# A sum of positive parts along rows: SyncE holds back its third and later loads until its first load has landed

## The chip, the cores and the metric

The kernel runs on one core of a Trainium2 chip. Five engines matter in different measure here: SyncE issues every transfer, ScalarE (ACT in the profile) and VectorE (DVE) compute, GpSimd (POOL) only sets four constants before the work begins, and TensorE does nothing. Transfers are carried by 16 DMA engines that all serve one queue. The metric is the time of one execution on the device, in microseconds (us); lower is better.

## The reference

The input has 32 x 512 rows of 1024 fp32 numbers, 64 MiB in all. Each row is cut at zero and summed.

```python
def reference(x: np.ndarray) -> np.ndarray:
    relu_x = np.maximum(x, 0)
    return np.sum(relu_x, axis=-1).astype(np.float32)
```

The result is 16,384 numbers, 64 KiB.

## The kernel before

The 16,384 rows are dealt to 128 partitions, 128 rows to each, in three regions (`REGIONS`, line 8): 1 row per partition, then 111, then 16. Within a region the rows of one partition are neighbours in memory. `xv` and `ov` (lines 45 to 49) are the views of input and output by region. A row of one partition is 4 KB, so "one row of each partition" is a load of 512 KB.

**Buffers.** `buf` has room for three buffers (`NB`) of 16 rows per partition (`BIG`), 8 MiB each. Big chunk `c` goes to buffer `c % 3`. There are seven big chunks, 0 to 6, and then 16 rows per partition of tail, cut into loads of 8, 4 and 2 rows and four pieces of the last two rows. Chunk 0 is the only one that is fetched by two loads (`CHUNKS`, line 9): first one row of each partition (512 KB, region 0), then 15 rows (7680 KB, region 1). Chunks 1 to 6 are one load of 16 rows each.

**SyncE's order (lines 85 to 123).** SyncE issues the loads in the order of the chunks, and the order is written out by hand. The two loads of chunk 0 are moved in the instruction list ahead of SyncE's arrival at the barrier with which all engines begin (lines 79 to 84, 95 to 97). Behind the barrier come chunks 1 and 2, with nothing to wait for, and from chunk 3 on a wait at line 87 until VectorE is through with the buffer that is to be refilled. The same wait stands ahead of the tail's loads. After those SyncE waits for results and issues the three stores. A semaphore `s_in[c]` counts 16 for each load that has landed; chunk 0's two loads share `s_in[0]`, so that its consumers wait for 32 (`16 * len(CHUNKS[c])`, lines 140 and 152).

**ScalarE and VectorE (lines 137 to 169).** For chunks 0 to 5 ScalarE cuts rows at zero in place in groups (`ACT_STEPS`), raising `s_act`, and VectorE sums the groups that ScalarE has finished (`DVE_STEPS`, line 160), raising `s_dve`, which frees the buffer. In chunk 0 this is one ScalarE instruction over all 16 rows and three reduces on VectorE. In chunks 4 and 5 some rows are left out of this pairing, and each engine does cut and sum of a row in a single instruction (`on_act`, `on_dve`, lines 126 to 132). Chunk 6 and the tail are done in that way throughout, with ScalarE and VectorE taking turns by rows (lines 173 to 185). The last row pair is cut at the element `CUT` and its pieces are gathered by sums in `seam` (lines 187 to 203). The output's last part is stored once both engines are done (line 207).

ScalarE needs its function table loaded ahead of its first ACTIVATE. No line of the kernel before asks for it; the compiler puts it in, and the profile shows it under line 145.

Of the kernel before, what the change touches and what calls it, by code (L numbers as in the profile page):

```python
# [8 lines left out]
CHUNKS = [[(0, 0, 1), (1, 0, 15)]] + [[(1, 16 * c + 15, 16)] for c in range(6)]  # L9
# [7 lines left out]
def bass_relu_sum_kernel(  # L17
# [16 lines left out]
    AF = mybir.ActivationFunctionType  # L34
# [21 lines left out]

    n_in = NBIG + len(TAIL) + 3
    s_in = [nc.alloc_semaphore(f"s_in{i}") for i in range(n_in)]
    s_act = nc.alloc_semaphore("s_act")
    s_dve = nc.alloc_semaphore("s_dve")  # L60
    s_fact = nc.alloc_semaphore("s_fact")
# [8 lines left out]
    sp, act, dve = nc.sync, nc.scalar, nc.vector  # L70
# [12 lines left out]
        if ins.engine == mybir.EngineType.SP and type(ins).__name__ == "InstDrain"  # L83
    )
    for c in range(NBIG + 1):
        if c >= NB:
            sp.wait_ge(s_dve, done[c - NB])
        if c < NBIG:
            i = 0
            for g, j, n in CHUNKS[c]:  # L90
                sp.dma_start(  # L91
                    out=buf[:, c % NB, i : i + n, :], in_=xv[g][:, j : j + n, :]
                ).then_inc(s_in[c], 16)
                i += n
                if c == 0:
                    code.insert(arrival, code.pop())
                    arrival += 1
# [28 lines left out]
    def on_act(t, acc):  # L126
        return act.activation(t, t, AF.Relu, accum_out=acc)  # L127

    def on_dve(t, acc):
        return dve.tensor_scalar(  # L130
            out=t, in0=t, scalar1=0.0, scalar2=None, op0=ALU.max, op1=ALU.add, accum_out=acc
        )

    def row(c, i):
        return buf[:, c % NB, i, :], res[:, c * BIG + i : c * BIG + i + 1]

    k = 0
    for c in range(NTWO):
        alone = BIG - sum(ACT_STEPS[c])
        act.wait_ge(s_in[c], 16 * len(CHUNKS[c]))  # L140
        r = 0
        ready = []
        for n in ACT_STEPS[c]:
            t = buf[:, c % NB, r : r + n, :]
            act.activation(t, t, AF.Relu).then_inc(s_act, 1)  # L145
            k += 1
            ready += [k] * n
            r += n
        for i in range(BIG - alone // 2, BIG):
            on_act(*row(c, i))  # L150
        if alone:
            dve.wait_ge(s_in[c], 16 * len(CHUNKS[c]))
            for i in range(BIG - alone, BIG - alone // 2):
                on_dve(*row(c, i))
        r = seen = 0
        for n in DVE_STEPS[c]:
            if ready[r + n - 1] > seen:
                seen = ready[r + n - 1]
                dve.wait_ge(s_act, seen)
            dve.tensor_reduce(  # L160
                out=res[:, c * BIG + r : c * BIG + r + n],
                in_=buf[:, c % NB, r : r + n, :],
                axis=X,
                op=ALU.add,
            ).then_inc(s_dve, 1)
            r += n
        if c == 1:
            dve.wait_ge(s_dve, done[c])
            dve.transpose(out=turned[:, :], in_=res[:, 0:32]).then_inc(s_turn, 1)  # L169
# [1 line left out]

    j0 = NBIG * BIG
    for c in range(NTWO, NBIG):
        act.wait_ge(s_in[c], 16 * len(CHUNKS[c]))
        dve.wait_ge(s_in[c], 16 * len(CHUNKS[c]))
        for i in range(BIG):
            ins = (on_act if i % 2 else on_dve)(*row(c, i))
            if i >= BIG - 2:
                ins.then_inc(s_fact if i % 2 else s_fdve, 1)
# [58 lines left out]
```

## Time and profile before

| what | value |
|---|---|
| median of 3 runs | 160.77 us |
| lowest and highest of them | 160.72 and 160.92 us |
| span of the profiled execution, first to last instruction | 159.4 us |
| VectorE busy | 120.6 us (76%) |
| ScalarE busy | 101.5 us (64%) |
| data queue, share of 16 DMA engines over the span | 98.1% |
| bytes read from HBM | 67.11 MB |

The page gives no whole time for the profiled execution, so its span stands beside the median of the runs that were timed. A span counts from the first instruction, here SyncE's first load, to the last. In the profile "SPq" is SyncE as it issues transfers; an issue is not counted as busy time of an engine, and its landing comes later. In a timeline a row gives its start, its length, the engine, the line, the operation and its tiles, and in brackets the idle time ahead of it and what ended that. In the table of stretches each row has the stretch, its length, the busy time of VectorE, ScalarE and GpSimd with their counts, the granted TensorE clock, the mean busy share of the 16 DMA engines and the GB/s that they moved. A packet is counted in a short stretch when it begins, so that shares over 1 are possible there.

### The profile page before, as it was taken

The page shows a single profiled execution, that of the slowest core. Times are in us where ns is not written, and L with a number is a line of the kernel's source. Part 1 is how long each engine was busy: PE and PEld are TensorE (multiplying, and loading weights), DVE is VectorE, ACT ScalarE, POOL GpSimd, SP SyncE. Part 2 cuts the span into 40 slices and gives each one's busy share as a digit, 9 for nine tenths or more (in the row PEclk, how much of TensorE's full clock was granted, in tenths as well). Part 3 has the DMA queues.
Part 4 walks back from the last instruction along what each step waited for, and adds up shares of the span by engine and source line. Part 5 has one row for each costly group of instructions (what it writes and reads, how often), then busy time and mean ns, then how long its engine had stood idle before and what let it go on. Part 6 is the DMA issues. An engine that isn't in the chain of part 4 may idle for free.

```text
span 159.4 us, 150 instructions
## 1 busy us (share of the span) xinstructions
DVE 120.6 (76%) x59; ACT 101.5 (64%) x54; POOL 0.2 (0%) x4
## 2 busy tenths in 40 slices
DVE  0000000009999999999999999999999999898995
ACT  3000059980799708996099941999329980496975
POOL 0000000000000000000000000000000000000000
DMA  9997996996996997989979969969969979798994
GB/s 378 493 401 339 493 526 263 526 526 263 526 493 296 526 444 345 526 378 411 526 312 477 526 263 526 526 263 526 526 263 526 444 345 526 321 469 374 417 400 142
DMA packets 2457, 67.18 MB, mean 421 GB/s; under 512 B 536, under 2 KB 792, under 8 KB 1176
## 3 DMA queue, kind: packets, MB, share of 16 engines
q1 hardware_dynamic: 2456, 67.18, 98.1%
q14 instruction: 1, 0.01, 0.0%
HBM read 67.11 MB, written 0.07 MB: 421 GB/s over the span
## 4 chain that ended last, share of the span: by engine, by line
DVE 55%; DMA 34%; ACT 9%; SPq 2%; issue 0%
DVE res L160 54%; DMA buf<-in_x_dram 34%; ACT buf L145 9%; SPq L101 1%; SPq L112 1%; DVE buf L130 0%; DVE seam L130 0%; SPq L91 0%; DVE turned L169 0%
## 5 line engine op out<-in xcount | busy, mean ns | idle before, releaser
L160 DVE TENSOR_REDUCE res<-buf 128x4 f32<-128x4096 f32 (+3 forms) x18 | 99.4, 5596 | 35.5 <-ACT buf L145 35.5
L145 ACT ACTIVATE buf<-buf 128x7168 f32<-128x7168 f32 (+5 forms) x13 | 80.4, 6233 | 46.1 <-DMA buf<-in_x_dram 46.1
L127 ACT ACTIVATE buf<-buf 128x1024 f32<-128x1024 f32 (+2 forms) x19 | 19.0, 999 | 8.9 <-DMA buf<-in_x_dram 8.9
L130 DVE TENSOR_SCALAR_CACHE_REDUCE buf<-buf 128x1024 f32<-128x1024 f32 (+2 forms) x19 | 20.7, 1143 | 1.7 <-DMA buf<-in_x_dram 1.6
L127 ACT ACTIVATION_READ_ACCUMULATOR buf<-buf 128x1 f32 x19 | 3.6, 188 | 0.0
L145 ACT ACT_TABLE_LOAD x1 | 1.3, 1283 | 1.3 <-PEq L223 1.3
L130 DVE DVE_READ_ACCUMULATOR buf<-buf 128x1 f32 x19 | 1.6, 84 | 0.0
L130 DVE TENSOR_SCALAR_CACHE_REDUCE seam<-seam 128x258 f32<-128x258 f32 x1 | 0.4, 421 | 0.0
L127 ACT ACTIVATE seam<-seam 128x114 f32<-128x114 f32 x1 | 0.3, 300 | 0.1
L169 DVE STREAM_TRANSPOSE turned<-res 128x32 f32<-128x32 f32 x1 | 0.2, 211 | 0.0
L127 ACT ACTIVATION_READ_ACCUMULATOR seam<-seam 128x1 f32 x1 | 0.2, 186 | 0.0
L223 POOL MEMSET const-bfloat16-1.0<- 128x1 bf16 x1 | 0.1, 101 | 0.0
L223 POOL MEMSET const-uint8-127<- 128x1 uint8 x1 | 0.1, 101 | 0.0
L223 POOL MEMSET const-float32-0.0<- 128x1 f32 x1 | 0.1, 98 | 0.2 <-issue 0.2
L223 POOL MEMSET const-float32-1.0<- 128x1 f32 x1 | 0.1, 98 | 0.0
L130 DVE DVE_READ_ACCUMULATOR seam<-seam 128x1 f32 x1 | 0.1, 82 | 0.0
## 6 DMA issues: line engine op xcount, KB each, us to landing
buf<-in_x_dram SPq DMA_DIRECT2D x1, 7680.0 KB, 21.1
buf<-in_x_dram SPq DMA_DIRECT2D x1, 4096.0 KB, 25.3
buf<-in_x_dram SPq DMA_DIRECT2D x1, 2048.0 KB, 29.9
buf<-in_x_dram SPq DMA_DIRECT2D x1, 1024.0 KB, 31.9
buf<-in_x_dram SPq DMA_DIRECT2D x1, 512.0 KB, 3.3
buf<-in_x_dram SPq DMA_DIRECT2D x1, 456.0 KB, 32.5
buf<-in_x_dram SPq DMA_DIRECT2D x1, 256.0 KB, 32.7
seam<-in_x_dram SPq DMA_DIRECT2D x1, 184.0 KB, 32.6
```

Of the source, the lines that this page charges most:

```text
L101: sp.dma_start(out=buf[:, tb, r : r + n, :], in_=xv[-1][:, r : r + n, :]).then_inc(s_in[NBIG + i], 16)
L112: sp.dma_start(out=flat[:, lo:hi], in_=rows[:, lo:hi]).then_inc(s_in[NBIG + len(TAIL) + k], 16)
L127: return act.activation(t, t, AF.Relu, accum_out=acc)
L130: return dve.tensor_scalar(out=t, in0=t, scalar1=0.0, scalar2=None, op0=ALU.max, op1=ALU.add, accum_out=acc)
L145: act.activation(t, t, AF.Relu).then_inc(s_act, 1)
L160: dve.tensor_reduce(out=res[:, c * BIG + r : c * BIG + r + n], in_=buf[:, c % NB, r : r + n, :], axis=X, op=ALU.add,).then_inc(s_dve, 1)
L169: dve.transpose(out=turned[:, :], in_=res[:, 0:32]).then_inc(s_turn, 1)
L223: nc = _bacc.Bacc("TRN2", target_bir_lowering=False, num_devices=1)
```

## The change

Load one of chunk 0, the single row of each partition, gets a semaphore of its own, `s_row`. SyncE waits for it ahead of chunk 1, and so ahead of every later load. ScalarE's table load is now asked for by name, ahead of a wait for `s_row` that stands in front of all of ScalarE's work. As each `s_in[c]` now counts one load only, its consumers wait for 16.

```diff
+    s_row = nc.alloc_semaphore("s_row")
...
     for c in range(NBIG + 1):
+        if c == 1:
+            sp.wait_ge(s_row, 16)
         if c >= NB:
             sp.wait_ge(s_dve, done[c - NB])
...
-                ).then_inc(s_in[c], 16)
+                ).then_inc(s_in[c] if i or c else s_row, 16)
...
+    act.preload_act_table(AF.Relu)
+    act.wait_ge(s_row, 16)
     k = 0
     for c in range(NTWO):
         alone = BIG - sum(ACT_STEPS[c])
-        act.wait_ge(s_in[c], 16 * len(CHUNKS[c]))
+        act.wait_ge(s_in[c], 16)
...
         if alone:
-            dve.wait_ge(s_in[c], 16 * len(CHUNKS[c]))
+            dve.wait_ge(s_in[c], 16)
...
     for c in range(NTWO, NBIG):
-        act.wait_ge(s_in[c], 16 * len(CHUNKS[c]))
-        dve.wait_ge(s_in[c], 16 * len(CHUNKS[c]))
+        act.wait_ge(s_in[c], 16)
+        dve.wait_ge(s_in[c], 16)
```

## The prediction

> **What bounds the kernel now.** I read the page's head and its table of DMA queues first, then the table of stretches cut at the landings of the big loads, then the chain of work that ended last, then the timeline of ScalarE and SyncE and the idle gaps of VectorE.
>
> ```profile
> span 159.4 us, 150 instructions
> DVE 120.6 (76%) x59; ACT 101.5 (64%) x54; POOL 0.2 (0%) x4
> q1 hardware_dynamic: 2456, 67.18, 98.1%
> ```
>
> The one data queue keeps its 16 engines busy for 98.1% of the span; VectorE is busy for 76%. The stretches (us, DVE, ACT, POOL busy, PE clock, DMA share, GB/s) say where that holds:
>
> ```profile
> 21.60:40.90 19.30, 5.40 (x2) 13.86 (x1) 0.00 (x0) 1.00 1.00 435
> 40.90:60.30 19.40, 19.40 (x4) 13.95 (x2) 0.00 (x0) 1.00 1.00 432
> 60.30:79.60 19.30, 19.27 (x6) 13.95 (x2) 0.00 (x0) 1.00 1.00 435
> ```
>
> From 21.6 us on, an 8 MB load takes one stretch of 19.3 to 19.4 us whatever the engines do: VectorE works 5.4 us of one and all of the next, and the rate stays. The chain that ended last seems to tell something else:
>
> ```profile
> 0.45 21.14 DMA buf<-in_x_dram
> 21.61 13.87 ACT buf L145
> 35.50 34.59 DVE res L160 x6
> 70.33 51.73 DVE res L160 x9
> 122.07 0.33 SPq L101
> 124.39 32.60 DMA buf<-in_x_dram
> ```
>
> It walks back from the last landing to the instruction that released its issue, VectorE's work. But a load issued at 124.4 that lands at 157.0, 32.6 us for 128 KB, was queueing behind other loads. The queue, not VectorE, is the bound. The waits by line confirm it from the consumers: both wait for data at each stage, and VectorE's wait is never over 0.5 us.
>
> ```profile
> ACT buf L145 <- DMA buf<-in_x_dram: 46.1, 6, 19.1
> DVE buf L130 <- DMA buf<-in_x_dram: 1.6, 4, 0.5
> ```
>
> The start is the only stretch where the queue is not yet full; the timelines of SyncE and ScalarE show it:
>
> ```profile
> 1.27 0.33 SPq L91 DMA_DIRECT2D buf<-in_x_dram  x1
> 1.27 1.28 ACT L145 ACT_TABLE_LOAD   x1 [1.27 <-PEq L223]
> 21.61 13.86 ACT L145 ACTIVATE buf<-buf 128x16384 f32<-128x16384 f32 x1 [19.06 <-DMA buf<-in_x_dram]
> 40.97 13.95 ACT L145 ACTIVATE buf<-buf 128x7168 f32<-128x7168 f32 x2 [5.50 <-DMA buf<-in_x_dram]
> buf<-in_x_dram SPq DMA_DIRECT2D x1, 7680.0 KB, 21.1
> buf<-in_x_dram SPq DMA_DIRECT2D x1, 512.0 KB, 3.3
> ```
>
> SyncE issues load one (512 KB) at 0.00, two (7680 KB) at 0.45, three at 1.27, four at 1.65. Load one lands at 3.3 us. Load two keeps the queue until 21.6, and load three lands at 40.9, one full stretch later.
>
> **The change, step by step.** The sum is made against the profiled execution: its span of 159.4 us. The page gives no whole time for that execution, so I set the median of 160.77 beside it; the 1.4 us between them lies outside the first and last instruction, where no step of the change acts, and is carried over.
>
> Load three waits (line 86). Load one has landed at 3.32 us. SyncE's wake-up after a releaser costs 0.03 us (VectorE's reduce ends at 52.84, the load it releases is issued at 52.86). So load three is issued at about 3.35 instead of 1.27, 2.1 us later. From the first issue to the first bytes is 1.0 us (DMA share 0.00 from 0 to 1 us), up to 1.4 us on the last engine by the trace's packet records. Load three's descriptors are there by 3.35 + 1.4 = 4.8 us, and the queue reaches them when load two is through, about 21.0. The cover is load two's 18 us of queued bytes, with 16 us left over. Were that cover gone, the step would cost the 2.1 us whole. Value 0; the row that fits best is load five, issued at 52.86 while load four runs and needed at 60.3, with no loss in stretches either side.
>
> What is queued behind the waiting instruction: load four (1.65 to about 3.73, needed at 40.9), then the wait for VectorE's three reduces of buffer 0 (52.84 us, so 49 us away). ScalarE waits for loads three and four only at 40.97 and 60.31. Cost 0.
>
> The Trainium skill, page "DMA: Bandwidth & Descriptors", section "Rules for kernel authors", speaks against this change: issue a DMA early and wait late, so that its fixed cost (about 2.0 us there) overlaps. By that rule two late loads with bare fixed costs would make 160.77 + 4.0 = 164.8; the trace's stretches after 40.9 us, where every load is issued late, show none of it, so the sum goes by them.
>
> ScalarE's part: a wait on the new semaphore and an explicit table load. The wait is over at 3.3 us and the first ACTIVATE is released at 21.6, so it has 18.3 us of cover. The table load is the one that already runs from 1.27 to 2.55 and stays ahead of the wait. If it ran after the first landing it would end at 3.35 + 1.28 = 4.6: still 0. The dropped count of 32 on a shared semaphore becomes 16 on each of two: same moment, 21.6. The one extra semaphore adds no instruction on any engine's row of work. 0.
>
> What the move may shift is contention. Descriptors of loads three and four now reach the engines after load one, not beside it.
> - The gain is at most what stage one loses. In the packet records 10 of the 16 engines have one 4 KB packet of load one at 0.25 to 0.34 us instead of 0.16, between 1.74 and 2.24 us: up to 0.18 on one engine. Load two takes 21.59 - 3.32 = 18.27 us; 15/16 of a stretch of 19.35 is 18.14, so 0.13 is lost there. Together 0.31.
> - The loss: two issues beside the running 60 KB packets. At 122.1 to 125.3 us seven loads are issued, and the 64 KB packets then in flight take 0.05 and 0.03 us over their 2.42: 0.08 for seven, 0.02 for two. Worst row: the first 60 KB packets, up to 0.21 over their 2.27, twice: 0.42.
> - Value: load five's issue, which changes two of 16 packets by 0.016 us and stretches by 0.02 us; that is the same kind of load at the same place in a running load. The gain I put at the same 0.02, since packets at 5 and 7.4 us, long after the last issue, are also up to 0.28 late, so the early stalls do not need these issues. Both ends go into the range.
>
> Sum: 0 (load three) + 0 (load four and SyncE) + 0 (ScalarE) - 0.02 + 0.02 = 0. Span 159.4, time 160.77 us. A difference of 0.2%, 0.32 us, is about what a measurement of this kernel can tell from no change (the three runs lie within 0.20).
>
> **The rivals.**
> *Stage one gets cleaner.* If the queued descriptors cause the early stalls, the 0.31 above comes back: 160.46, still inside the bound. To pass it, the skew of the engines must shrink too: load one's 16 engines land from 2.81 to 3.32, and the last load's still from 156.98 to 157.44, so the last engine's late start is paid at the end. With half of that 0.51 also gone: 160.77 - 0.31 - 0.25 = 160.2. For it: that the skew persists for 154 us. Against it: the engines' first packets start 0.35 us apart before load three is issued, and the change does not touch that.
>
> *The late issues disturb load two.* This one ends slower: loads three and four meet 16 engines in the middle of 60 KB packets, and each costs the last engine the worst row, 0.21: 160.77 + 0.42 = 161.19. It decides from 0.16 us per load on. For it: the packets of 2.5 us, in flight as the descriptors of the old issues came, are the long ones. Against it: load five's 0.016 us and the tail's 0.01 per load.
>
> *ScalarE's table is loaded twice,* once more behind the 21.6 us landing. Then ScalarE and VectorE run 1.28 us late. VectorE ends its reduces at 137.3 + 1.28 = 138.6, and its waits for data, 0.42, 0.51 and 0.24 us, and 0.15 more ahead of 154.84, absorb 1.32: 160.77. Loads five to eight and the tail are issued 1.28 later; the tightest is load five, at 54.1 + 1.4 = 55.5 for a queue that is free at 60, with 4.5 us to spare. No change either.
>
> *The wait never binds.* It would need load one to have landed by 1.27; it lands at 3.3. Then 160.77 as well.
>
> **How the numbers follow.** No measurable change, with either harmless rival: 0.80, its own range 160.55 to 161.0 from the spread of the runs (0.20) round the median. Cleaner start beyond 0.32 us: 0.10, as half of it needs a skew that the change does not reach. Disturbed load two beyond 0.32 us: 0.10, as it needs ten times load five's row. Faster, same, slower: 0.10, 0.80, 0.10. The range goes from 160.45, the whole early loss regained, to 161.1, most of the worst row twice; the two rivals' tenths lie outside it.
>
> **What the changed profile would show.** Load three's issue at 3.35 instead of 1.27; load four's at 3.7; the first ACTIVATE still at 21.6 and the second at 40.97; stretches of 19.35 unchanged; one table load before 3 us. Wrong would be: the first ACTIVATE moved by more than 0.1 us, earlier (the stalls did come from the queued issues) or later (the late issues disturb). A gap in the DMA share near 21 us would mean that issue to first bytes is far longer under load than 1.4 us. A stretch other than 19.35 later on would mean the engines' order or skew sets the rate, which nothing here shows.

## The result and the profile after

The changed kernel is slower by a fifth of a per cent: 161.16 us (median of 22 runs, 160.76 to 161.53) against 160.80 us (22 runs, 160.72 to 161.03), a ratio of 1.0019 with a 95% interval of 1.0013 to 1.0024. No change was predicted, and 161.16 also lies above the range's end of 161.1.

The profile of the changed kernel shows none of this. Head, data queue, and the stretches between the landings of the big loads (same columns as before):

```profile
span 159.4 us, 151 instructions
q1 hardware_dynamic: 2456, 67.18, 98.0%
```

```profile
21.60:40.90 19.30, 5.31 (x2) 13.86 (x1) 0.00 (x0) 1.00 1.00 435
40.90:60.30 19.40, 19.40 (x3) 13.95 (x2) 0.00 (x0) 1.00 1.00 432
60.30:79.60 19.30, 19.27 (x6) 13.95 (x2) 0.00 (x0) 1.00 1.00 435
```

The span is 159.4 us again and the stretches are the same. One thing is new: 151 instructions instead of 150. The timelines of SyncE and ScalarE show the change at its place:

```profile
3.33 0.33 SPq L94 DMA_DIRECT2D buf<-in_x_dram  x1
1.26 1.28 ACT L140 ACT_TABLE_LOAD   x1 [1.26 <-PEq L228]
21.70 13.86 ACT L150 ACTIVATE buf<-buf 128x16384 f32<-128x16384 f32 x1 [19.16 <-DMA buf<-in_x_dram]
40.99 13.95 ACT L150 ACTIVATE buf<-buf 128x7168 f32<-128x7168 f32 x2 [5.43 <-DMA buf<-in_x_dram]
```

Load three is issued at 3.33 instead of 1.27 and the second chunk is taken up at 40.99 instead of 40.97. The first ACTIVATE starts 0.09 us later. The chain of work shows the new instruction just ahead of it, a ScalarE instruction of its own for one of the two waits:

```profile
21.64 0.02 ACTq L145
21.65 0.05 issue
21.70 13.87 ACT buf L150
```

The waits of the consumers (engine, line, releaser; us in total, times, longest) show that this does not reach the end: VectorE's wait for data is 1.6 us in total, as before:

```profile
ACT buf L150 <- DMA buf<-in_x_dram: 46.1, 6, 19.2
DVE buf L133 <- DMA buf<-in_x_dram: 1.6, 5, 0.5
```

So I looked at what each run has outside its span. Every run lists its time and its span, the latter to 0.1 us. In the runs of the kernel before on the next chip (35 of them) the time less the span is 1.31 to 1.42 us, mean 1.365. In the 22 runs of the changed kernel it is 1.40 to 1.97, mean 1.67: nine are at 1.40 to 1.46, thirteen at 1.71 to 1.97. The spans have a mean of 159.45. **The 0.3 us lie outside the first and last instruction.** The profiled execution is one of the nine, with 160.83 us.

The trace also holds the semaphore events behind the last instruction: a first closing barrier, the reset of the semaphores, and a second barrier. The profile's page does not print them, and the events name no engine: a barrier is read from nine updates of one semaphore, which come in the same pattern ahead of the program. In ns from the first event after the end, the second barrier reads

```
kernel before:   987 1021 1059 1103 1126 | 1223 1262 1296 1343
changed kernel:  992 1074 1112 1155 1179 | 1277 1315 1350 1396
```

I read the first five as the engines' arrivals and the rest as the way back. The second arrival comes 82 ns after the first instead of 34, and everything behind it is late by the same 48 ns. That is the 0.04 us which even a short execution has: with the trace's spans, which are given to the nanosecond, the profiled executions of this program length are at 1.40 to 1.42 outside, those of the length before (e3 to e5 below) at 1.36 to 1.38.

### The profile page after: what moved, and what is told of

It reads as the page before. It is cut to its first block, busy times and chain, and to the rows that moved or that the text cites. A ratio compares the mean times of both kernels' runs of the same rounds, so it can differ in the third digit from the quotient of the medians.

```text
span 159.4 us, 151 instructions
## 1 busy us (share of the span) xinstructions
DVE 120.6 (76%) x59; ACT 101.5 (64%) x54; POOL 0.2 (0%) x4
## 4 chain that ended last, share of the span: by engine, by line
DVE 55%; DMA 34%; ACT 9%; SPq 2%; issue 0%; ACTq 0%
DVE res L165 54%; DMA buf<-in_x_dram 34%; ACT buf L150 9%; SPq L104 1%; SPq L115 1%; DVE buf L133 0%; DVE seam L133 0%; SPq L94 0%; DVE turned L174 0%; ACTq L145 0%
```

## The experiments

All were timed beside the kernel before on the same chip; e1 to e4, e5 to e8, f1 to f4 and the g's each had a chip of their own. A result gives the median time, the ratio to the kernel before with its 95% interval, and "outside", which is the time less the span, as a mean over the runs. A figure in ns is the second arrival in the second closing barrier, counted from the first, in the profiled execution. Theory A puts the time inside the program (A1: SyncE's late issues; A2: ScalarE's wait). B puts it outside, by the extra semaphore. L puts it outside, by the length of ScalarE's program. W holds that it takes the wait for the row at ScalarE's start.

**The changed kernel once more** (e1).

> The changed kernel once more, as the yardstick for the others. The runs shown so far have 161.16 us against 160.80, yet spans of 159.3 to 159.6 on both sides. If the time was added inside the program (theory A: the two late issues disturb load two, or ScalarE's extra wait delays the start), a profile with a long time must show a first ACTIVATE later than 21.70 by 0.3 us or more. If it is added outside the first and last instruction (theory B), the span stays at 159.4 to 159.5 while the time is 161.0 to 161.3.

160.92 us, ratio 1.0009 (1.0000 to 1.0017). Outside 1.48 against 1.365: two of 12 runs at 1.72 and 2.0, the others at 1.38 to 1.46. The span's mean is 159.49 against 159.48. The late arrival is there again (82 ns). The time is outside the program, which speaks against A in both forms; how many executions are long differs from chip to chip (13 of 22, then 2 of 12).

**All but SyncE's wait** (e2).

```diff
-        if c == 1:
-            sp.wait_ge(s_row, 16)
```

> All of the change but SyncE's wait: load one has its own semaphore, ScalarE waits for both, loads three and four are issued at 1.27 and 1.65 us again. If SyncE's wait is the cause (A1), the time is back at 160.8. If ScalarE's extra wait instruction or the extra semaphore is the cause (A2, B), it stays at 161.1 to 161.2.

160.99 us, ratio 1.0010 (1.0001 to 1.0018); outside 1.54, three of 11 at 1.88 or 1.89; late arrival 83 ns. The cost is there without SyncE's wait: A1 falls.

**SyncE's wait without the rest** (e3).

```diff
+    s_row = nc.alloc_semaphore("s_row")
...
+        if c == 1:
+            sp.wait_ge(s_row, 1)
...
+    act.preload_act_table(AF.Relu).then_inc(s_row, 1)
```

> SyncE's wait without the rest: both loads of chunk 0 count on one semaphore as before, ScalarE has no added wait; SyncE holds loads three and four until ScalarE's table load has ended, at about 2.6 us instead of 3.33. If late issues are the cause (A1), 161.0 to 161.2, perhaps less as the delay is 1.3 us and not 2.1. If ScalarE's extra wait (A2) is, 160.8. If the extra semaphore is (B), 161.1.

Load three is issued at 2.57:

```profile
2.57 0.33 SPq L94 DMA_DIRECT2D buf<-in_x_dram  x1
```

160.85 us, ratio 1.0003 (0.9995 to 1.0012); outside 1.375, none over 1.42; second arrival 34 ns. SyncE's delay of 1.3 us costs nothing that shows, and neither does a table load that is asked for by name, or a semaphore more.

**A semaphore more, unused** (e4).

> The kernel before with one more semaphore allocated at the same place and never used, so that the numbers of the semaphores behind it move up by one. If the numbering or count of semaphores costs time outside the program (B), 161.1. Under A1 and A2, 160.8.

160.84 us, ratio 1.0001 (0.9992 to 1.0009); outside 1.36; 34 ns. B in the form of the semaphores' numbers falls. What e2 has and e3 and e4 lack is ScalarE's extra instruction.

**The changed kernel with one ScalarE instruction saved elsewhere** (e5).

```diff
-    on_act(flat[:, lo : CUT // 2], seam[:, 0:1]).then_inc(s_half, 1)
-    on_dve(flat[:, CUT // 2 : hi], seam[:, 1:2]).then_inc(s_half, 1)
+    on_act(flat[:, lo : CUT // 2], seam[:, 0:1]).then_inc(s_seam, 1)
+    on_dve(flat[:, CUT // 2 : hi], seam[:, 1:2]).then_inc(s_seam, 1)
...
-    act.wait_ge(s_seam, 16 + 2)
-    act.wait_ge(s_half, 2)
+    act.wait_ge(s_seam, 16 + 4)
...
-    dve.wait_ge(s_seam, 16 + 2)
+    dve.wait_ge(s_seam, 16 + 4)
```

> The changed kernel with one wait instruction of ScalarE saved at the end: the increments of the semaphore for the halves go to the seam's semaphore, so one wait for 20 replaces two. SyncE's wait, the new semaphore and ScalarE's two waits at the start stay. Theory L (the length of ScalarE's program: one instruction more moves what ScalarE runs after the kernel's end, and the time comes after the last instruction): time less span back to 1.36 in every run, and in the semaphore events after the end the second arrival of the second closing barrier is back at 0.034 us behind the first, where the changed kernel has 0.082. Theory W (the wait for the row at ScalarE's start itself): both stay at 1.40 and above, and 0.082.

```profile
span 159.4 us, 150 instructions
```

150 instructions again, and 160.76 us, ratio 0.9996 (0.9988 to 1.0005); outside 1.35, none over 1.40; 34 ns. With the whole change in place, wait for the row included, the cost is gone. W falls.

**The kernel before with an unrelated wait more on ScalarE** (e6).

```diff
+        if c == 2:
+            act.wait_ge(s_dve, 1)
         act.wait_ge(s_in[c], 16 * len(CHUNKS[c]))
```

> The kernel before with one more wait instruction on ScalarE, ahead of chunk 2, for something long true (VectorE's first reduce). No SyncE wait, no new semaphore. Theory L: 0.082 in the closing barrier, time less span at 1.40 with some runs at 1.7 to 2.0. Theory W: 0.034 and 1.36, as before.

160.84 us in the median, ratio 1.0009 (1.0000 to 1.0018). Outside 1.53: three of 11 at 1.78 to 1.90, one at 1.36, seven at 1.42 to 1.44; 78 ns. It has the marks of e1, with nothing of the change in it. L's forecast came true; how it works was the next question.

**Four such waits** (e7), ahead of chunks 2 to 5.

```diff
+        if c >= 2:
+            act.wait_ge(s_dve, c - 1)
         act.wait_ge(s_in[c], 16 * len(CHUNKS[c]))
```

> As the one before, but with one such wait ahead of each of chunks 2 to 5, four instructions more on ScalarE. Theory L in a form in which each instruction costs: time less span at 1.36 + 4 x 0.04 = 1.5. In a form in which ScalarE's program crosses a boundary at which code is fetched: the late arrival is there, of the size of e1's or larger, and the share of runs at 1.7 and above is at least as high. Theory W: 1.36.

160.81 us, ratio 1.0000 (0.9991 to 1.0009); outside 1.36, none over 1.41; 35 ns. More instructions, no cost: neither of the forms of L that I had written down. W had forecast this number, but e5 and e6 speak against W. So it is not a price per instruction, and it is not worse past a boundary: a length can be bad, and a longer one good.

**A wait more on VectorE** (e8).

```diff
+                if c == 2 and r == 0:
+                    dve.wait_ge(s_in[0], 16 * len(CHUNKS[0]))
                 dve.wait_ge(s_act, seen)
```

> The kernel before with one more wait instruction on VectorE, ahead of chunk 2's first reduce, for something long true (both loads of chunk 0). If any engine's longer program costs time after the end, 1.40 and above here too. If it is only ScalarE's (L: its program alone lies at a boundary), 1.36 and 0.034 in the closing barrier.

Outside 1.36, none over 1.39; 34 ns. VectorE's program could grow by one at no cost outside the span. (160.86 us, ratio 1.0006, 0.9997 to 1.0015: the mean span was 159.56 here against 159.48, a difference that I leave open.)

**The changed kernel with three waits more** (f1), ahead of chunks 3 to 5, so that ScalarE has four instructions more than before the change.

```diff
+        if c >= 3:
+            act.wait_ge(s_dve, c - 1)
         act.wait_ge(s_in[c], 16)
```

> The changed kernel with three more wait instructions on ScalarE, ahead of chunks 3 to 5, for something long true: four more than the kernel before. If the length of ScalarE's program decides (L, with a place that is bad and others that are not), the added work makes the kernel faster than the changed one: time less span 1.36 in every run, 0.034 in the closing barrier, 160.8. If the change's own parts matter (W, or SyncE's wait), 1.40 and above stays, and three waits more can't help.

160.79 us, ratio 1.0000 (0.9991 to 1.0009); outside 1.36, none over 1.43; 34 ns. Three useless waits repair the changed kernel. It was not timed as it stands on this chip; the firmer sign is the second arrival, which is 77 to 84 ns in all eight profiles with one instruction more and 34 ns here.

**Two and three waits** (f2, f3), as e7 with chunks 2 to 3 and 2 to 4.

> The kernel before with two more wait instructions on ScalarE (ahead of chunks 2 and 3). One more was bad (time less span 1.42 to 1.9, late arrival 0.078), four more were not (1.36, 0.034, and a code fetch of 8 KB that begins ahead of the end, at 159.0). L: this one falls on either side and tells where the bad place ends; if bad, some of the runs at 1.7 and above; if not, the early fetch at 159.0 is there.

> As the one before with three more. L: if two are harmless, so are three; if two are bad, this shows whether the bad place is two or three instructions wide. 1.36 with an early fetch at about 159.0, or 1.40 and above without.

f2: 161.01 us, ratio 1.0014 (1.0005 to 1.0023), outside 1.55 (1.38 to 1.68). f3: 160.96 us, ratio 1.0010 (1.0001 to 1.0019), outside 1.50 (1.39 to 1.57). Both are bad in another way than e6: no late arrival (35 and 36 ns) and no run above 1.68, but most above 1.45. The bad place is three instructions wide on this side.

**One ScalarE instruction fewer** (f4): the edit of e5 on the kernel before.

> The kernel before with one wait instruction of ScalarE saved at the end (one semaphore for seam and halves), nothing of the change. With SyncE's wait in the changed kernel the same edit gave 160.76. L: 1.36 and 0.034, 160.8. If SyncE's wait has a gain of its own that ScalarE's longer program hid, this one stays at 160.84 and is 0.07 above that; if the saved instruction gave it, 160.76.

```profile
span 159.5 us, 149 instructions
```

160.96 us, ratio 1.0010 (1.0001 to 1.0019): shorter is slower too. Outside 1.52, every run at 1.46 to 1.56. This time the second barrier is late on its way back (ns, as above):

```
f4:  987 1021 1059 1103 1127 | 1224 1262 1419 1466
```

The third step back takes 157 ns instead of 34. I had expected 1.36; the bad place has another side.

**A ScalarE instruction that is no wait** (g2): an ACTIVATE of one element per partition in ScalarE's idle time.

```diff
+    pad = nc.alloc_sbuf_tensor("pad", [P, 1], fp32)
...
+        if c == 2:
+            act.activation(pad[:, :], nc.const_aps.scalar_like(0.0, pad[:, :]), AF.Relu)
```

> The kernel before with one more instruction on ScalarE that is no wait: an ACTIVATE of one element per partition from a constant to a scratch tile, ahead of chunk 2. It takes some 0.2 us in ScalarE's idle time. L, if the count of instructions decides: time less span 1.40 and above with some long ones, late arrival of 0.08 in the closing barrier, as with one more wait. If it takes a wait: 1.36 and 0.034.

161.12 us, ratio 1.0020 (1.0008 to 1.0033); outside 1.64, five of 10 at 1.76 to 1.97; 78 ns. It does not take a wait: an ACTIVATE does it too. This is the changed kernel's result with a ScalarE instruction of no use in place of the change.

**Three more profiles of kernels with one instruction more** (g1, g3, g4: the changed kernel, e6 and e2), each in search of a long execution.

> The changed kernel, one look, for a profile of a long execution. If the time is over 161.0 with a span of 159.4 to 159.5, theory L says that the whole excess stands in the semaphore events after the last instruction, at one arrival or release of the second closing barrier (0.3 to 0.6 us in one step where the others take 0.03 to 0.1), and that nothing ahead of the first instruction has grown. If the excess were ahead of the first instruction, L falls.

> The kernel before with one wait more on ScalarE ahead of chunk 2, one look, for a profile of a long execution. As for g1: long only after the last instruction (L), or else ahead of the first.

> The change without SyncE's wait, one look, for a profile of a long execution. As for g1.

All three were short: 160.81, 160.89 and 160.76 us, outside 1.40 to 1.41 by the trace's spans, with the late arrival of 77 to 84 ns. A miss: no profile of a long one was had.

Put together by the number of ScalarE's instructions, outside in us:

| ScalarE instructions against before | kernels | outside, mean | second arrival |
|---|---|---|---|
| -1 | f4 | 1.52 | 34 ns (way back 0.12 late) |
| 0 | before, e3, e4, e5, e8 | 1.35 to 1.375 | 34 ns |
| +1 | changed, e1, e2, e6, g2 (arrival: g1, g3, g4 too) | 1.48 to 1.67 | 77 to 84 ns |
| +2 | f2 | 1.55 | 35 ns |
| +3 | f3 | 1.50 | 36 ns |
| +4 | e7, f1 | 1.36 | 34 to 35 ns |

What each program does inside plays no part that shows: e5 and e3 have SyncE's wait, e2 and e6 have not.

The traces also say how much of the time outside the span the closing events account for. In the fourteen profiled executions with 0, 1 or 4 instructions more whose time is on record, the time outside is 0.09 to 0.11 us less than the interval from the last instruction to the last closing event: the 0.04 us of the short ones with one instruction more is the late arrival, whole. In f4 the late way back accounts for 0.12 of 0.14 us. In f2 and f3 it is otherwise. Their closing events are on time, and yet the time outside is 0.05 and 0.12 us longer than that interval, so 0.15 and 0.22 us lie beyond what these events show.

What lies behind the count is hinted at by a queue that the profile names "instruction" (q14), by which I take it to carry the engines' code. In the table of queues, which covers the span, f1 with four instructions more has two of its packets, of 8 KB each; the kernel before has one:

```profile
q14 instruction: 2, 0.02, 0.1%
```

The stretch from 157 us to 162 us shows where. Its rows are the busy tenths and the GB/s of 40 slices of 0.125 us; 8 KB in a slice are 66 GB/s, so a code fetch is a slice at 66 to 68, from 159.0 us on. The kernel before, one fetch:

```profile
DMA  0000000383000052020000000000000000000000
GB/s 0 0 0 0 0 0 0 99 252 103 0 0 0 0 47 19 0 66 0 0 0 0 0 0 0 0 0 0 0 0 0 0 0 0 0 0 0 0 0 0
q14 instruction: 1, 0.01, 0.6%
```

f1, a second one ahead of it, at 159.08 and so before the program's end:

```profile
DMA  0000000077100015304000000000000000000000
GB/s 0 0 0 0 0 0 0 14 210 210 22 0 0 0 17 47 68 0 66 0 0 0 0 0 0 0 0 0 0 0 0 0 0 0 0 0 0 0 0 0
q14 instruction: 2, 0.02, 1.7%
```

f2, the second one behind it, at 160.72, in the closing sequence:

```profile
DMA  0000000185000033003000000000020000000000
GB/s 0 0 0 0 0 0 0 50 256 146 4 0 0 0 36 30 0 0 66 0 0 0 0 0 0 0 0 0 0 66 0 0 0 0 0 0 0 0 0 0
q14 instruction: 2, 0.02, 1.3%
```

With four more (e7, f1) the second fetch begins before the end and costs nothing that shows. With two or three it begins 1.19 and 1.15 us after the first closing event, and it is all that the trace has there to set beside their 0.15 and 0.22 us. With -1, 0 and +1 the trace has no second fetch at all. A reading that fits is that the length decides where in the closing sequence ScalarE's code runs into its next block. It is argued and not shown: the records do not say whose code a packet carries, and for +1 and -1 no fetch is recorded.

## Why the prediction was wrong

**The step that failed** is the frame of the sum: "The 1.4 us between them lies outside the first and last instruction, where no step of the change acts, and is carried over." The change acts there, by one ScalarE instruction; the term is 1.67 us in the 22 runs where I carried over 1.4. The step beside it helped it to fail: "ScalarE's part" was costed by its cover of 18.3 us, as a wait that is long over, and the sum counted no instruction for it. Two waits ahead of one ACTIVATE made a separate wait instruction: the trace has three semaphore instructions of ScalarE instead of two. I said that the extra semaphore adds no instruction, and that is true (e4); the extra wait does. The bounds from both sides were drawn for the contention of transfers alone, so the range had no room for this term: 161.16 lies 0.06 above it, and the 0.10 given to slower was for a rival that the runs speak against. None of the signs of being wrong that the prediction named could have caught this, as all of them lie inside the span; the first ACTIVATE, 0.09 us late, stayed within its 0.1.

**What was right.** Load three at 3.35 and load four at 3.7: 3.33 and 3.71. That it costs nothing: e3 with 1.0003, e5 with 0.9996 and f1 with 1.0000, all with SyncE's wait, each with an interval of under 0.1% to either side. The terms of -0.02 and +0.02 us are too small for these runs to show. Nor is a gain of the wait shown: e5's spans are 0.06 us shorter than those of the kernel before beside it (159.42 against 159.48), but so are those of e6, which has no wait of SyncE. Stretches of 19.35: landings 19.32 to 19.38 apart. One table load before 3 us: yes, at 1.26. The first ACTIVATE was to stay at 21.6 and came at 21.70: 0.03 of it is the landing (21.62 against 21.59), the rest the new instruction, and ScalarE's idle time of over 5 us in the next stage takes it up. As load two was to be slowed or quickened by a wait, I measure it from load one's landing: 18.30 to 18.41 us in the six profiles with SyncE's wait, 18.19 to 18.47 in the twelve without it. The wait moves nothing that shows.

**Two readings that were off,** without effect on the sum. VectorE does not wait for data at each stage: all of its four waits for data come after 137 us, and from 35.5 to 137.3 us it runs on without one, in the second stretch for 19.40 of 19.40 us. In those stages the queue and VectorE are both full. And nine 4 KB packets of load one, not ten, took 0.25 us or more between 1.74 and 2.24 us.

**The rivals.** "Stage one gets cleaner" and "the late issues disturb load two" both fall by these numbers: neither 0.31 us less nor 0.42 more is there. The early stalls do not come from the queued issues either. In the changed kernel eight of load one's packets take 0.25 to 0.39 us between 1.58 and 2.25 us, when loads three and four have not been issued. The table is loaded once. The wait binds: SyncE's table of waits has it at 2.1 us.

```profile
SPq L94 <- DMA buf<-in_x_dram: 2.1, 1, 2.1
```

**The skill's rule.** The Trainium skill's page "DMA: Bandwidth & Descriptors", section "Rules for kernel authors", has a load issued early so that its fixed cost overlaps; the prediction estimated 164.8 for late issues from it. Here two issues that are 2.1 us late cost nothing that shows (e3, e5, f1), with some 16 us of queued bytes ahead of them by the prediction's estimate; no run here takes that cover away.

**What stays open.** Where the 0.3 to 0.6 us of the long executions lie. None of the eight profiles of kernels with one ScalarE instruction more was of a long one. The spans of the long executions, to 0.1 us, exclude the inside, but behind the end or ahead of the start is not told apart. That it is behind the end, at the arrival which is late by 0.04 to 0.05 us in all eight, is likely and not shown. How ScalarE's length moves these events is open too, as is why 13 of 22 executions were long on one chip and 2 of 12 on another.

## What to carry to other kernels

When a kernel is tuned to a few tenths of a microsecond, compare the time less the span too: a change that leaves the span as it was can still cost time outside it, here 0.04 to 0.6 us for one ScalarE instruction that was itself hidden. Before such a change is judged, test it at other program lengths, by an instruction saved or some useless ones added on the same engine; here the change gave 1.0019 and 1.0009 as it stood, 0.9996 with an instruction saved and 1.0000 with three added. And count instructions, not waits: a second wait ahead of one instruction was an instruction of its own here, while the waiting itself cost nothing.

## What the runs showed that was not expected

The time outside the span is sensitive to ScalarE's length downwards as well as upwards: one instruction fewer costs 0.15 us in the mean and 0.08 or more in each of 11 runs, one more 0.04 us or 0.3 to 0.6, two 0.18, three 0.12, four nothing. One instruction more on VectorE changed nothing there.

The Trainium skill's page "Runtime: NRT & Kernel Launch", section "Instruction fetch mechanics", says of crossing a block boundary of an engine's code that its cost is "mostly hidden". For a fetch that begins before the program's end (e7, f1: 1.36 us outside) the runs agree. Where one is recorded in the closing sequence (f2, f3: 1.55 and 1.50) time was lost, and the measurement decides, though that the fetch is the cause is not shown. Its blocks are of 16 KiB; the packets that this trace records are of 8 KB.
